# Rectify and sum rows of 1024: two of seven large loads issued from ScalarE's queue, with other step lengths for two of them

## The chip, the core and the metric

The kernel runs on one core of one Trainium2 chip. The time is the device time of one execution in microseconds (us), and the median of three runs is compared. The core has engines that work side by side, each with its own instruction stream[...]: here ScalarE (ACT in the profile), VectorE (DVE) and SyncE (SP), which computes nothing and issues transfers. TensorE has no work, and GpSimd (POOL) only sets four constants at the start. Sixteen DMA engines carry the transfers between memory (HBM) and the core's own memory of 128 partitions.

## The reference

```python
def reference(x):                       # x: 32 x 512 x 1024, float32
    relu_x = np.maximum(x, 0)
    return np.sum(relu_x, axis=-1).astype(np.float32)    # 32 x 512
```

There are 16,384 rows of 1024 numbers, 67.1 MB in all. Of each row the positive numbers are summed.

## The kernel before

The rows are dealt to 128 partitions, 128 rows to each. The tile `buf` holds three buffers of 16 rows per partition (64 KB per partition, 8 MB in all), and `res` the 128 sums of each partition.

The input comes in seven chunks of 16 rows per partition (`CHUNKS`, c0 to c6), then in a tail of smaller loads: 8, 4 and 2 rows (`TAIL`), and the last two rows in four pieces. c0 consists of a load of one row and one of fifteen. Each of c1 to c6 is one load whose piece in each partition is 64 KB of contiguous memory. Chunk c goes to buffer c mod 3.

All loads are issued by SP, in order, at L91 (chunks), L101 (`TAIL`), L112 and L115 (last pieces), on one queue. The first three chunks go out at once. From c3 on, L87 makes SP wait until VectorE has finished with the chunk that held the buffer: `done[c]` is the number of VectorE's reductions up to the end of chunk c, and `s_dve` counts them. So c3 waits for `done[0]`, c4 for `done[1]`, c5 for `done[2]`, c6 for `done[3]`, and the tail for `done[4]`. Each load counts up its own semaphore `s_in[c]` when it lands.

Chunks c0 to c5 are worked by two engines one after the other (loop at L138). ScalarE waits for `s_in[c]`, then rectifies the chunk in place (L145) in steps of so many rows as `ACT_STEPS[c]` says, each counting `s_act`. VectorE sums the rectified rows (L160) in steps of `DVE_STEPS[c]` rows; each step waits for the first of ScalarE's steps that cover all its rows. Two reductions can thus wait for two different steps of one chunk. Where the steps of ScalarE cover fewer than 16 rows (c5: 12), the other four are `alone` rows: ScalarE does two and VectorE two, each rectifying and summing in one instruction (`on_act` L127, `on_dve` L130). After c1 a small transpose (L169) prepares the first 128 sums for storing.

c6 and the tail are not split into two stages: there the engines take rows in turn with `on_act` and `on_dve`, so each row is done by one instruction. The last sums are then stored by SP (L207), and the program ends when they are in memory.

Of the kernel before, what the change touches and what calls it, by code (L numbers as in the profile page):

```python
# [6 lines left out]
NB = 3  # L7
REGIONS = [1, 111, 16]
CHUNKS = [[(0, 0, 1), (1, 0, 15)]] + [[(1, 16 * c + 15, 16)] for c in range(6)]
ACT_STEPS = [[16], [7, 9], [7, 9], [7, 9], [4, 5, 7], [3, 4, 5]]  # L10
DVE_STEPS = [[4, 5, 7], [7, 4, 5], [7, 4, 5], [7, 4, 5], [4, 5, 7], [3, 4, 5]]
TAIL = [8, 4, 2]
CUT = 912
HEAD = 256
# [2 lines left out]
def bass_relu_sum_kernel(  # L17
    nc: bass.Bass,
    x: bass.AP,
    out: bass.AP,  # L20
):

# [20 lines left out]
    xv = [  # L45
        xr[P * s : P * (s + n), :].rearrange("(p j) d -> p j d", p=P)
        for s, n in zip(start, REGIONS)
    ]
    ov = [of[P * s : P * (s + n)].rearrange("(p j) -> p j", p=P) for s, n in zip(start, REGIONS)]

    buf = nc.alloc_sbuf_tensor("buf", [P, NB, BIG, D], fp32)
# [6 lines left out]
    s_in = [nc.alloc_semaphore(f"s_in{i}") for i in range(n_in)]  # L58
    s_act = nc.alloc_semaphore("s_act")
    s_dve = nc.alloc_semaphore("s_dve")  # L60
# [9 lines left out]
    sp, act, dve = nc.sync, nc.scalar, nc.vector  # L70

    NTWO = len(ACT_STEPS)
    done = [sum(map(len, DVE_STEPS[: c + 1])) for c in range(NTWO)]

# [8 lines left out]
        if ins.engine == mybir.EngineType.SP and type(ins).__name__ == "InstDrain"  # L83
    )
    for c in range(NBIG + 1):
        if c >= NB:
            sp.wait_ge(s_dve, done[c - NB])  # L87
        if c < NBIG:
            i = 0
            for g, j, n in CHUNKS[c]:  # L90
                sp.dma_start(  # L91
                    out=buf[:, c % NB, i : i + n, :], in_=xv[g][:, j : j + n, :]
                ).then_inc(s_in[c], 16)
                i += n
                if c == 0:
                    code.insert(arrival, code.pop())
                    arrival += 1
# [13 lines left out]
    for k, (lo, hi) in enumerate((first, second, third)):  # L111
# [6 lines left out]
        out=of[0:P].rearrange("(k q) -> k q", q=32), in_=turned[0:P:32, 0:32]  # L118
# [7 lines left out]
    def on_act(t, acc):  # L126
        return act.activation(t, t, AF.Relu, accum_out=acc)  # L127

    def on_dve(t, acc):
        return dve.tensor_scalar(  # L130
            out=t, in0=t, scalar1=0.0, scalar2=None, op0=ALU.max, op1=ALU.add, accum_out=acc
        )

    def row(c, i):
        return buf[:, c % NB, i, :], res[:, c * BIG + i : c * BIG + i + 1]

    k = 0
    for c in range(NTWO):  # L138
        alone = BIG - sum(ACT_STEPS[c])
        act.wait_ge(s_in[c], 16 * len(CHUNKS[c]))  # L140
        r = 0
        ready = []
        for n in ACT_STEPS[c]:
            t = buf[:, c % NB, r : r + n, :]
            act.activation(t, t, AF.Relu).then_inc(s_act, 1)  # L145
            k += 1
            ready += [k] * n
            r += n
        for i in range(BIG - alone // 2, BIG):
            on_act(*row(c, i))  # L150
        if alone:
            dve.wait_ge(s_in[c], 16 * len(CHUNKS[c]))
            for i in range(BIG - alone, BIG - alone // 2):
                on_dve(*row(c, i))
        r = seen = 0
        for n in DVE_STEPS[c]:
            if ready[r + n - 1] > seen:
                seen = ready[r + n - 1]
                dve.wait_ge(s_act, seen)
            dve.tensor_reduce(  # L160
                out=res[:, c * BIG + r : c * BIG + r + n],
                in_=buf[:, c % NB, r : r + n, :],
                axis=X,
                op=ALU.add,
            ).then_inc(s_dve, 1)
            r += n
        if c == 1:
            dve.wait_ge(s_dve, done[c])
            dve.transpose(out=turned[:, :], in_=res[:, 0:32]).then_inc(s_turn, 1)  # L169
# [68 lines left out]
```

## Time and profile before

| | |
|---|---|
| median of three runs | 160.91 us (160.76 to 160.96) |
| the profiled execution | 160.74 us |
| its span in the profile | 159.4 us |
| bytes moved | 67.18 MB, mean 421 GB/s |
| ScalarE's wait for the first chunk | 19.1 us |
| VectorE's wait for ScalarE's first step | 35.5 us |
| ScalarE's waits for all six chunks | 46.1 us |
| last store, issue to landing | 1.4 us |

The span is what the profiler saw of the program, and 1.34 us of the measured time lie around it. In the profile a line begins with the place in the code (L160), then comes the engine, the operation, what it writes and reads, and how often. A row of the timeline begins with start and duration in us; at its end stands the idle time before it and what ended that. `SPq` is SP's issuing of a transfer[...]; the transfer itself runs on the DMA engines. A digit of a row of slices is the busy share of one fortieth of the span in tenths. Queue `q1` is the one that SP issues on.

### The profile page before, as it was taken

Reading aid. Unit: us, or ns where it says so; the run is one execution under the profiler, and the core shown is the slowest. Engines: PE = TensorE matmul, PEld = TensorE weight load, DVE = VectorE, ACT = ScalarE, POOL = GpSimd, SP = SyncE. Lnnn points to the kernel's source line nnn. Section 1 sums busy time; section 2 is a strip of 40 time slices with the busy share of each in tenths; the row PEclk is TensorE's granted clock in tenths of the full one; section 3 lists DMA queues with packets and bytes.
Section 4 is the critical chain, followed back from the end, with each engine's and each line's share of the span. In section 5 each row is a group of like instructions: output and inputs, shape, how many; then the busy total and the mean of one; then the engine's idle time right before and its main releaser. Section 6 shows DMA issues by size and latency. Waiting matters only on the chain.

```text
span 159.4 us, 150 instructions
## 1 busy us (share of the span) xinstructions
DVE 120.6 (76%) x59; ACT 101.5 (64%) x54; POOL 0.2 (0%) x4
## 2 busy tenths in 40 slices
DVE  0000000009999999999999999999999999898995
ACT  3000059980799708996099941999329980496975
POOL 0000000000000000000000000000000000000000
DMA  9997996996996997989979969969969979798994
GB/s 378 493 401 339 493 526 263 526 526 263 526 493 296 526 444 345 526 378 411 526 312 477 526 263 526 526 263 526 526 263 526 444 345 526 321 469 374 417 400 142
DMA packets 2457, 67.18 MB, mean 421 GB/s; under 512 B 536, under 2 KB 792, under 8 KB 1176
## 3 DMA queue, kind: packets, MB, share of 16 engines
q1 hardware_dynamic: 2456, 67.18, 98.1%
q14 instruction: 1, 0.01, 0.0%
HBM read 67.11 MB, written 0.07 MB: 421 GB/s over the span
## 4 chain that ended last, share of the span: by engine, by line
DVE 55%; DMA 34%; ACT 9%; SPq 2%; issue 0%
DVE res L160 54%; DMA buf<-in_x_dram 34%; ACT buf L145 9%; SPq L101 1%; SPq L112 1%; DVE buf L130 0%; DVE seam L130 0%; SPq L91 0%; DVE turned L169 0%
## 5 line engine op out<-in xcount | busy, mean ns | idle before, releaser
L160 DVE TENSOR_REDUCE res<-buf 128x4 f32<-128x4096 f32 (+3 forms) x18 | 99.4, 5596 | 35.5 <-ACT buf L145 35.5
L145 ACT ACTIVATE buf<-buf 128x7168 f32<-128x7168 f32 (+5 forms) x13 | 80.4, 6233 | 46.1 <-DMA buf<-in_x_dram 46.1
L127 ACT ACTIVATE buf<-buf 128x1024 f32<-128x1024 f32 (+2 forms) x19 | 19.0, 999 | 8.9 <-DMA buf<-in_x_dram 8.9
L130 DVE TENSOR_SCALAR_CACHE_REDUCE buf<-buf 128x1024 f32<-128x1024 f32 (+2 forms) x19 | 20.7, 1143 | 1.7 <-DMA buf<-in_x_dram 1.6
L127 ACT ACTIVATION_READ_ACCUMULATOR buf<-buf 128x1 f32 x19 | 3.6, 188 | 0.0
L145 ACT ACT_TABLE_LOAD x1 | 1.3, 1283 | 1.3 <-PEq L223 1.3
L130 DVE DVE_READ_ACCUMULATOR buf<-buf 128x1 f32 x19 | 1.6, 84 | 0.0
L130 DVE TENSOR_SCALAR_CACHE_REDUCE seam<-seam 128x258 f32<-128x258 f32 x1 | 0.4, 421 | 0.0
L127 ACT ACTIVATE seam<-seam 128x114 f32<-128x114 f32 x1 | 0.3, 300 | 0.1
L169 DVE STREAM_TRANSPOSE turned<-res 128x32 f32<-128x32 f32 x1 | 0.2, 211 | 0.0
L127 ACT ACTIVATION_READ_ACCUMULATOR seam<-seam 128x1 f32 x1 | 0.2, 186 | 0.0
L223 POOL MEMSET const-bfloat16-1.0<- 128x1 bf16 x1 | 0.1, 101 | 0.0
L223 POOL MEMSET const-uint8-127<- 128x1 uint8 x1 | 0.1, 101 | 0.0
L223 POOL MEMSET const-float32-0.0<- 128x1 f32 x1 | 0.1, 98 | 0.2 <-issue 0.2
L223 POOL MEMSET const-float32-1.0<- 128x1 f32 x1 | 0.1, 98 | 0.0
L130 DVE DVE_READ_ACCUMULATOR seam<-seam 128x1 f32 x1 | 0.1, 82 | 0.0
## 6 DMA issues: line engine op xcount, KB each, us to landing
buf<-in_x_dram SPq DMA_DIRECT2D x1, 7680.0 KB, 21.1
buf<-in_x_dram SPq DMA_DIRECT2D x1, 4096.0 KB, 25.3
buf<-in_x_dram SPq DMA_DIRECT2D x1, 2048.0 KB, 29.9
buf<-in_x_dram SPq DMA_DIRECT2D x1, 1024.0 KB, 31.9
buf<-in_x_dram SPq DMA_DIRECT2D x1, 512.0 KB, 3.3
buf<-in_x_dram SPq DMA_DIRECT2D x1, 456.0 KB, 32.5
buf<-in_x_dram SPq DMA_DIRECT2D x1, 256.0 KB, 32.7
seam<-in_x_dram SPq DMA_DIRECT2D x1, 184.0 KB, 32.6
```

What stands on the lines that cost most here:

```text
L101: sp.dma_start(out=buf[:, tb, r : r + n, :], in_=xv[-1][:, r : r + n, :]).then_inc(s_in[NBIG + i], 16)
L112: sp.dma_start(out=flat[:, lo:hi], in_=rows[:, lo:hi]).then_inc(s_in[NBIG + len(TAIL) + k], 16)
L127: return act.activation(t, t, AF.Relu, accum_out=acc)
L130: return dve.tensor_scalar(out=t, in0=t, scalar1=0.0, scalar2=None, op0=ALU.max, op1=ALU.add, accum_out=acc)
L145: act.activation(t, t, AF.Relu).then_inc(s_act, 1)
L160: dve.tensor_reduce(out=res[:, c * BIG + r : c * BIG + r + n], in_=buf[:, c % NB, r : r + n, :], axis=X, op=ALU.add,).then_inc(s_dve, 1)
L169: dve.transpose(out=turned[:, :], in_=res[:, 0:32]).then_inc(s_turn, 1)
L223: nc = _bacc.Bacc("TRN2", target_bir_lowering=False, num_devices=1)
```

## The change

The loads of c3 and c5 (the fourth and the sixth chunk) are no longer issued by SP but by ScalarE, on its own queue. SP's loop leaves them out, its wait with them. In ScalarE's stream the load of chunk c + 2 stands after the rectifying steps of chunk c: c3's after those of c1, c5's after those of c3. Each has the same condition as before, a wait for `done[c - 1]` of the loop (`done[0]` for c3, `done[2]` for c5), and counts the same semaphore at landing. c4, c6 and the tail remain with SP and their waits.

The steps of two chunks change. c3 is rectified in one step of 16 rows instead of two (7 and 9); c4 in two (7, 9) instead of three (4, 5, 7). VectorE's steps for c3 and c4 are exchanged accordingly. The number of reductions in each chunk stays three, so `done` keeps its values, and the work done on each row stays the same.

```diff
-ACT_STEPS = [[16], [7, 9], [7, 9], [7, 9], [4, 5, 7], [3, 4, 5]]
-DVE_STEPS = [[4, 5, 7], [7, 4, 5], [7, 4, 5], [7, 4, 5], [4, 5, 7], [3, 4, 5]]
+ACT_STEPS = [[16], [7, 9], [7, 9], [16], [7, 9], [3, 4, 5]]
+ON_ACT = (3, 5)
+DVE_STEPS = [[4, 5, 7], [7, 4, 5], [7, 4, 5], [4, 5, 7], [7, 4, 5], [3, 4, 5]]
...
     for c in range(NBIG + 1):
+        if c in ON_ACT:
+            continue
         if c >= NB:
             sp.wait_ge(s_dve, done[c - NB])
...
             k += 1
             ready += [k] * n
             r += n
+        if c + 2 in ON_ACT:
+            [(g, j, n)] = CHUNKS[c + 2]
+            act.wait_ge(s_dve, done[c - 1])
+            act.dma_start(out=buf[:, (c + 2) % NB, :, :], in_=xv[g][:, j : j + n, :]).then_inc(
+                s_in[c + 2], 16
+            )
         for i in range(BIG - alone // 2, BIG):
             on_act(*row(c, i))
```

## The prediction

> **What bounds the kernel now.** I read the page's busy shares and slices first, then the chain of waits, then the timelines of SP's queue, ScalarE and VectorE, then the groups by shape.[...]
>
> ```profile
> span 159.4 us, 150 instructions
> DVE 120.6 (76%) x59; ACT 101.5 (64%) x54; POOL 0.2 (0%) x4
> DVE  0000000009999999999999999999999999898995
> ACT  3000059980799708996099941999329980496975
> q1 hardware_dynamic: 2456, 67.18, 98.1%
> ...
> 35.50 34.59 DVE res L160 x6
> 70.09 0.02 issue
> 70.11 0.21 DVE turned L169
> 70.33 51.73 DVE res L160 x9
> ...
> DVE buf L130 <- DMA buf<-in_x_dram: 1.6, 4, 0.5
> ```
>
> Two resources are full together. The 16 DMA engines carry packets for 98.1% of the span, and VectorE, once its first input is there at 35.50, works almost without a hole: the chain runs through its reductions for 86 us, and all its later waits sum to 1.6 us. So a hole of more than 1.6 us opened in VectorE after 35.5 us lengthens the run one for one, even if no byte comes later.
>
> ```profile
> 52.86 0.33 SPq L91 DMA_DIRECT2D buf<-in_x_dram  x1
> 70.11 0.33 SPq L91 DMA_DIRECT2D buf<-in_x_dram  x1
> 87.58 0.33 SPq L91 DMA_DIRECT2D buf<-in_x_dram  x1
> ...
> 40.97 13.95 ACT L145 ACTIVATE buf<-buf 128x7168 f32<-128x7168 f32 x2 [5.50 <-DMA buf<-in_x_dram]
> 60.31 13.95 ACT L145 ACTIVATE buf<-buf 128x7168 f32<-128x7168 f32 x2 [5.39 <-DMA buf<-in_x_dram]
> 79.67 13.95 ACT L145 ACTIVATE buf<-buf 128x7168 f32<-128x7168 f32 x2 [5.41 <-DMA buf<-in_x_dram]
> 99.02 14.04 ACT L145 ACTIVATE buf<-buf 128x4096 f32<-128x4096 f32 x3 [5.40 <-DMA buf<-in_x_dram]
> ...
> L160 DVE TENSOR_REDUCE res<-buf 128x7 f32<-128x7168 f32 x5 | 37.9, 7605 | 0.0
> L160 DVE TENSOR_REDUCE res<-buf 128x5 f32<-128x5120 f32 x6 | 32.9, 5480 | 0.0
> L160 DVE TENSOR_REDUCE res<-buf 128x4 f32<-128x4096 f32 x6 | 26.5, 4413 | 35.5 <-ACT buf L145 35.5
> L145 ACT ACTIVATE buf<-buf 128x16384 f32<-128x16384 f32 x1 | 13.9, 13856 | 19.1 <-DMA buf<-in_x_dram 19.1
> ```
>
> The SP lines are the issues of c3, c4 and c5. ScalarE starts each chunk when it lands, so its lines give the landings: c1 40.97, c2 60.31, c3 79.67, c4 99.02, one every 19.35 us. c3 is issued at 52.86, while c2 still has 7.4 us to go: on one queue it stands behind c2 and costs it nothing. A chunk is 64 KB in each of 128 partitions, eight per DMA engine, so one 64-KB piece takes 19.35/8 = 2.42 us.
>
> [...] (2)[...] 8.389 MB per 19.35 us is 433.5 GB/s, so a second queue has nothing left to win. (3)[...] No run here shows it yet; both cases are worked out.[...]
>
> **The change part by part.**
>
> 1. c3 moves to ScalarE's queue. With (3) it goes out at 52.86 as before, on done[0]. Start-up: the first 512 KB landed 3.3 us after issue, of which 0.5 MB at 433 GB/s is 1.2, so 2.1 us lie at both ends; I take 1.5 of it before the first byte (estimate), which makes 54.4. c2's pieces run from 60.2 - 19.35 = 40.85; at 54.4 its sixth is under way and ends at 55.4. Then in turns: c3's first to 57.8, c2's seventh to 60.2, c3's second to 62.6, c2's eighth to 65.0. c2 lands at 65.1 instead of 60.31.
>
> 2. c4 goes out on SP's queue at done[1], unmoved at 70.1; bytes from 71.6. c3 has been alone since 65.0 and its fifth piece ends at 72.3. Then c4, c3, c4, c3, c4, c3: the eighth of c3 ends at 72.3 + 6 x 2.42 = 86.8, and it lands at 87.0 instead of 79.67. That is three pieces, 7.3 us.
>
> 3. VectorE in c2: ScalarE's first step is done at 65.1 + 6.17 = 71.3, its second (7.87) at 79.2. VectorE is free at 70.33, waits 1.0, reduces seven rows to 78.9, waits 0.3, then 4.41 + 5.48 to 89.1 (before 87.58).
>
> 4. c3's rectifying becomes one step of 16 rows. Nothing can be reduced until all of it is done: 87.0 + 13.86 = 100.9. VectorE idles from 89.1 to 100.9, 11.8 us. Before, the seven-row step sufficed, 79.67 + 6.17 = 85.8, ahead of 87.58. The joining saves one ACTIVATE's fixed cost:[...] 13.95 against 13.86, so 0.09 us.
>
> 5. VectorE's holes: 1.0 + 0.3 + 11.8 = 13.1 us, against slack of 1.6: **+11.5 us**. The new orders (4,5,7 for c3, 7,4,5 for c4) sum to the same 17.5 us a chunk, cost nothing.
>
> 6. c5 on ScalarE's queue, and c4's steps [7,9]. c5 goes out at done[2] = 89.1 and shares with c4: bytes 90.7, turns from 91.7; c4 ends at 106.2, lands at 106.3 (before 99.02). ScalarE has its first step ready at 112.5 and its second at 120.4; VectorE, in c3 until 100.9 + 17.5 = 118.4, needs them at 118.4 and 126.0: hidden. c5's rest ends at 118.3.
>
> 7. c6 stays on SP, on done[3], now 118.4 instead of 104.8: bytes at 119.9, a DMA hole of 1.6 us; c6 lands near 139.4. The tail goes out at done[4], 135.9, before c6 is in. VectorE comes to c6 only at 150.4 to 151.0 (137.30, the end of its last c5 reduction, plus 13.1 to 13.7, as much as the sum of step 5 and the shift of done[3], 104.8 to 118.4, say), so all later landings are hidden by its own lateness. If c6 were later by over 11 us this would matter.
>
> 8. Two DMA issues on ScalarE's sequencer, 0.33 us each by SP's rows. What stands behind each is the next chunk's activation, which waits for a landing 8 us or more away: nothing.
>
> If instead the DMA waits until the activation before it has ended (against (3)): c3 out at 40.97 + 13.95 = 54.9, bytes at 56.5, inside c2's seventh piece; c2 lands at 62.7 and no longer holds VectorE, but c3 still ends at 86.8. VectorE idles from 87.6 to 100.9, 13.3 us, the same sum. c5 then goes out at 100.9 and the DMA stands for 3.5 us after c4's end at 98.9, hidden under VectorE's lateness, as in step 7. The time hardly tells the two apart.
>
> Sum: the profiled execution took 160.74 (span 159.4 and 1.34 around it). 160.74 + 11.5 = 172.2; the median of the runs, 160.91, is 0.17 above: **172.4**.
>
> Bounds of the unknown sharing: from below, no sharing at all (first come, first served). c3 lands at 79.67, is rectified at 93.5, VectorE waits from 87.6 to 93.5, 5.9 - 1.6 = +4.3: 165.2. Nothing lower while the rate stands: c2 and c3 together can't be in before 79.4, and if c3 is not the last of them, c2 is, and VectorE waits for it sooner and longer. From above, c3 goes first whenever it can: c3 in at 74, c2 last at 79.6, first reduction at 85.8 instead of 70.3: 15.5, and after it c3's step, ready at 107.4 against done[2] at 103.1, 4.3 more: +18.2, 179.
>
> **The rivals.**
>
> A, even turns, c3 three pieces late: 172.4. For it: 64-KB pieces standing in both queues[...].
> B, pieces of the old queue already taken in when the new one begins go first, so that c3 is one or two late: 165.2 + 2.42 or 4.84, 167.6 to 170.0.[...]
> C, whole loads in order of arrival: 165.2, all of it from the sixteen-row step.[...]
> D, ScalarE's queue gets more than half, or c3 is four pieces late: 174.8 to 179.
> E, not slower: two queues fill gaps that one leaves, so bytes come faster from 54 us on. It decides from the point where c3 is in by 87.58 + 1.6 - 13.86 = 75.3: 25 us of transfer in 20.9, 520 GB/s, with VectorE's floor 160.9 - 1.6 = 159.3. The slices of the page show single values near 526, but next to 263, so they are bookkeeping; the mean of 421 and (2) speak against it. 159.3 to 160.9.
>
> **How the numbers follow.** A 0.64, B 0.13, C 0.14, D 0.06, E 0.03. The likeliest gives 172.4. The range must take in C and B and an error of one piece above A (2.42): 164.8 to 175.0, with most of D and E left out. A measurement of this kernel tells 0.2% from no change; E is split 0.02 faster, 0.01 same, the rest is slower: 0.97.
>
> **What would show it.** Right: ScalarE starts c2 near 65 and c3 near 87; VectorE has one hole of 11 to 13 us ended by ScalarE's sixteen-row step near 101, none worth naming after it; one DMA queue more, holding 16.8 MB; the tail's waits for DMA gone from VectorE. If c2 starts at 60.3 and c3 at 79.7, C holds. If c5 goes out near 89, the sequencer ran ahead; near 101, it did not. Wrong altogether: c3 in by 75, or c2's landing past 70.

## The result, and the profile after

The changed kernel takes 171.97 us (median of four runs, 171.94 to 172.02) against 160.86 us before (four runs as well): a ratio of 1.069 (95% interval 1.068 to 1.071). The profiled execution took 171.97 us, with a span of 170.6 us. The forecast was 172.4 us in a range of 164.8 to 175.0.

These are lines of the page of the changed kernel, and below the dots its waits by engine (time in all, number of times, longest). Its lines L95, L149, L170 and L134 are L91, L145, L160 and L130 of before.

```profile
span 170.6 us, 148 instructions
DVE 120.5 (71%) x59; ACT 101.2 (59%) x52; POOL 0.2 (0%) x4
DVE  0000000069999999799980039999999999999996
ACT  3000099934998007995069960999999109987500
q1 hardware_dynamic: 2168, 50.40, 69.4%
q10 hardware_dynamic: 288, 16.78, 22.7%
...
DVE res L170 <- ACT buf L149: 48.6, 4, 35.5
```

VectorE is busy for as long as before (120.5 against 120.6 us) and the same bytes move, now 16.78 MB of them on a second queue, `q10`. The difference is a hole in VectorE's row of slices, the digits 80039, and a DMA share that fell from 98.1% to 92.1%. VectorE now waits four times for ScalarE instead of once, 48.6 us instead of 35.5: 13.1 us more. Its waits for the tail's loads, 1.6 us before, have gone from the list.

The timelines of the changed kernel, VectorE's above and ScalarE's below the dots (start, duration, what; in brackets the idle time before it and what ended that; `ACTq` is ScalarE's issuing of a load):

```profile
70.07 0.21 DVE L179 STREAM_TRANSPOSE turned<-res 128x32 f32<-128x32 f32 x1
71.39 7.62 DVE L170 TENSOR_REDUCE res<-buf 128x7 f32<-128x7168 f32 x1 [1.11 <-ACT buf L149]
79.16 9.81 DVE L170 TENSOR_REDUCE res<-buf 128x4 f32<-128x4096 f32 x2 [0.15 <-ACT buf L149]
100.84 34.58 DVE L170 TENSOR_REDUCE res<-buf 128x4 f32<-128x4096 f32 x6 [11.87 <-ACT buf L149]
...
52.83 0.38 ACTq L156 DMA_DIRECT2D buf<-in_x_dram  x1
65.18 13.95 ACT L149 ACTIVATE buf<-buf 128x7168 f32<-128x7168 f32 x2 [10.29 <-DMA buf<-in_x_dram]
86.95 13.86 ACT L149 ACTIVATE buf<-buf 128x16384 f32<-128x16384 f32 x1 [7.82 <-DMA buf<-in_x_dram]
89.01 0.33 ACTq L156 DMA_DIRECT2D buf<-in_x_dram  x1
106.30 24.47 ACT L149 ACTIVATE buf<-buf 128x7168 f32<-128x7168 f32 x5 [5.50 <-DMA buf<-in_x_dram]
```

Read ScalarE first. c2 starts at 65.18 instead of 60.31, c3 at 86.95 instead of 79.67, c4 at 106.30 instead of 99.02. c3 is rectified in one step of 13.86 us, so nothing of it can be summed before 100.81. VectorE is out of c2 at 88.97 and starts c3 at 100.84. After that it never waits again. The chain of waits of the changed kernel says the same in order of time:

```profile
52.83 34.10 DMA buf<-in_x_dram
86.93 0.02 issue
86.95 13.87 ACT buf L149
100.82 0.02 issue
100.84 34.58 DVE res L170 x6
```

The load of c3 alone, 34.1 us from issue to landing, carries the chain here. In the kernel before, the 86 us in the middle of the chain were VectorE's without a break.

### The profile page after: what moved, and what is told of

Read it like the earlier page. It is cut to its first block, busy times and chain, and to the rows that moved or that the text cites. A ratio compares the mean times of both kernels' runs of the same rounds, so it can differ in the third digit from the quotient of the medians.

```text
span 170.6 us, 148 instructions
## 1 busy us (share of the span) xinstructions
DVE 120.5 (71%) x59; ACT 101.2 (59%) x52; POOL 0.2 (0%) x4
## 3 DMA queue, kind: packets, MB, share of 16 engines
q10 hardware_dynamic: 288, 16.78, 22.7%
## 4 chain that ended last, share of the span: by engine, by line
DMA 43%; DVE 40%; ACT 15%; issue 0%
DMA buf<-in_x_dram 43%; DVE res L170 28%; ACT buf L149 15%; DVE buf L134 12%; DVE seam L134 0%
## 5 line engine op out<-in xcount | busy, mean ns | idle before, releaser
L170 DVE TENSOR_REDUCE res<-buf 128x4 f32<-128x4096 f32 (+3 forms) x18 | 99.7, 5596 | 48.6 <-ACT buf L149 48.6
L149 ACT ACTIVATE buf<-buf 128x7168 f32<-128x7168 f32 (+5 forms) x11 | 80.1, 7331 | 48.1 <-DMA buf<-in_x_dram 48.1
L134 DVE TENSOR_SCALAR_CACHE_REDUCE buf<-buf 128x1024 f32<-128x1024 f32 (+2 forms) x19 | 20.4, 1136 | 0.0
L134 DVE DVE_READ_ACCUMULATOR buf<-buf 128x1 f32 x19 | 1.5, 79 | 0.0
L134 DVE TENSOR_SCALAR_CACHE_REDUCE seam<-seam 128x258 f32<-128x258 f32 x1 | 0.4, 421 | 0.0
L134 DVE DVE_READ_ACCUMULATOR seam<-seam 128x1 f32 x1 | 0.1, 82 | 0.0
```

What stands on the lines that cost most here:

```text
L134: return dve.tensor_scalar(out=t, in0=t, scalar1=0.0, scalar2=None, op0=ALU.max, op1=ALU.add, accum_out=acc)
L170: dve.tensor_reduce(out=res[:, c * BIG + r : c * BIG + r + n], in_=buf[:, c % NB, r : r + n, :], axis=X, op=ALU.add,).then_inc(s_dve, 1)
```

## The experiments

All runs are of the changed kernel with the edit shown, except where the old step lengths are put back. Each was timed beside the kernel before on the same chip.

**Step lengths alone.**

```diff
-ON_ACT = (3, 5)
+ON_ACT = ()
```

> All loads on SP's queue again, only the new step lengths kept. Theory of turns (A): without a second queue c3 lands at 79.7 as before; the sixteen-row step ends at 93.5 and VectorE, free at 87.6, waits 5.9 us; less 1.6 us of slack gives 164.7 to 165.2. If instead the long step itself cost nothing and all the loss came from the second queue, 160.9.

165.12 us, ratio 1.026 (1.024 to 1.028). VectorE's timeline of this kernel:

```profile
70.24 17.30 DVE L170 TENSOR_REDUCE res<-buf 128x7 f32<-128x7168 f32 x3
93.54 34.58 DVE L170 TENSOR_REDUCE res<-buf 128x4 f32<-128x4096 f32 x6 [6.00 <-ACT buf L149]
```

There is one new hole, 6.00 us, at the place and of the size that the long step should give, with every landing where it was before. So part of the loss has nothing to do with queues.

**Second queue alone.**

```diff
-ACT_STEPS = [[16], [7, 9], [7, 9], [16], [7, 9], [3, 4, 5]]
+ACT_STEPS = [[16], [7, 9], [7, 9], [7, 9], [4, 5, 7], [3, 4, 5]]
...
-DVE_STEPS = [[4, 5, 7], [7, 4, 5], [7, 4, 5], [4, 5, 7], [7, 4, 5], [3, 4, 5]]
+DVE_STEPS = [[4, 5, 7], [7, 4, 5], [7, 4, 5], [7, 4, 5], [4, 5, 7], [3, 4, 5]]
```

> c3 and c5 on ScalarE's queue, the old step lengths. Theory A: ScalarE starts c2 at 65.2 and c3 at 87.0 as in the changed kernel, but its seven-row step is done at 93.1, so VectorE waits 1.1 + 0.2 + 4.1 us instead of 13.1; 5.4 less 1.6 gives about 164.6. If the steps carried the whole loss, 160.9; if the queue carried nearly all of it, 170 or more.

164.83 us, ratio 1.024 (1.022 to 1.025). VectorE's timeline:

```profile
71.40 7.62 DVE L170 TENSOR_REDUCE res<-buf 128x7 f32<-128x7168 f32 x1 [1.05 <-ACT buf L149]
79.17 9.81 DVE L170 TENSOR_REDUCE res<-buf 128x4 f32<-128x4096 f32 x2 [0.15 <-ACT buf L149]
93.17 7.62 DVE L170 TENSOR_REDUCE res<-buf 128x7 f32<-128x7168 f32 x1 [4.18 <-ACT buf L149]
100.94 27.07 DVE L170 TENSOR_REDUCE res<-buf 128x4 f32<-128x4096 f32 x5 [0.15 <-ACT buf L149]
```

c3 lands at 86.95 here too, but its first seven rows are ready at 93.1. Step lengths and queue cost 4.2 and 3.9 us alone (the kernel before took 160.93 us beside them) and 11.1 together. The surplus has a plain reason: the kernel before had two reserves that each half could use by itself, 1.6 us of VectorE's slack and the 1.7 us by which c3's first step (85.8) was ahead of VectorE (87.6). Together they can be spent only once: 4.2 + 3.9 + 1.6 + 1.7 is 11.4, against 11.1 measured.

**Loads that wait for ScalarE's own work.** One line is added ahead of the load in ScalarE's stream:

```diff
+            act.wait_ge(s_act, k)
             act.wait_ge(s_dve, done[c - 1])
```

> The changed kernel, but each load on ScalarE's queue waits for ScalarE's own earlier steps to end, so c3 goes out at 54.9 and c5 at 100.8 instead of 52.8 and 89.0. Theory (the sequencer's running ahead is worth nothing here): DMA stands about 3 us after c4, but VectorE comes to c6 only at 150, so 172.0, unchanged within 0.5. Rival: the hole in the transfers adds to the time, 174 to 176.

172.17 us, ratio 1.070 (1.068 to 1.071). The two issues moved to 55.01 and 100.87, and VectorE's one hole came to 13.26 us, ending at 100.87:

```profile
55.01 0.39 ACTq L157 DMA_DIRECT2D buf<-in_x_dram  x1
62.80 13.95 ACT L149 ACTIVATE buf<-buf 128x7168 f32<-128x7168 f32 x2 [7.82 <-DMA buf<-in_x_dram]
86.98 13.86 ACT L149 ACTIVATE buf<-buf 128x16384 f32<-128x16384 f32 x1 [10.24 <-DMA buf<-in_x_dram]
100.87 0.33 ACTq L157 DMA_DIRECT2D buf<-in_x_dram  x1
```

c2 comes 2.4 us sooner and c3 at the same moment as in the changed kernel, so the two small holes in c2 melt into the large one. An issue of c5 that is 12 us later is hidden by VectorE's lateness. Whether the loads go out during ScalarE's steps or after them makes little difference to the time (171.97 against 172.17 us).

**One of the two loads at a time.** `ON_ACT` is `(3,)` in the first run, `(5,)` in the second.

> Only c3 on ScalarE's queue; c5 is SP's again; new step lengths. Theory A: c5's place costs nothing since VectorE's hole is closed at 100.8 by c3 alone: 172.0, c4 landing at 99.0 again instead of 106.3. Rival: half of the loss belongs to c5's sharing with c4, about 166.

172.22 us, ratio 1.070 (1.068 to 1.071): with the new step lengths, c3's move by itself makes the whole loss. c4 is no longer held up (the DMA records have it in by 98.8 us), and that buys nothing.

> Only c5 on ScalarE's queue; c3 is SP's again; new step lengths. c3 lands at 79.7, the long step opens 5.9 us as with the steps alone (165.1); then c4 shares with c5 and lands at 106 to 109, its seven-row step is done at 112.5 to 115, VectorE is out of c3 at 111.0 and waits 1.5 to 4 more: 167 to 169. Rival: c5's move is free wherever it stands, 165.1.

169.25 us, ratio 1.052 (1.051 to 1.054), a little above the 167 to 169 us that were expected. VectorE's timeline:

```profile
93.64 17.34 DVE L170 TENSOR_REDUCE res<-buf 128x4 f32<-128x4096 f32 x3 [6.02 <-ACT buf L149]
114.97 7.62 DVE L170 TENSOR_REDUCE res<-buf 128x7 f32<-128x7168 f32 x1 [3.99 <-ACT buf L149]
```

So c5's move isn't harmless in itself: it delays c4 (ScalarE starts it at 108.76, with the step lengths alone at 99.00) as c3's delays c2, and costs 4.1 us over the step lengths alone. In the changed kernel it is free only because VectorE has already been made late enough by c3.

**How the DMA engines share.** Now the pieces of one of two loads that share the engines are made small. A chunk loaded as four loads of 4 rows has pieces of 16 KB instead of 64 KB; bytes, buffers and waits stay. First c3, on ScalarE's queue (its load becomes a loop over the four parts, issued one after the other):

```diff
+CHUNKS[3] = [(1, 16 * 2 + 15 + i, 4) for i in range(0, 16, 4)]
```

> The changed kernel with c3 as four loads of 4 rows, so 16-KB pieces against SP's 64-KB pieces; same bytes, same moments. If the DMA engines take turns by piece: c2 is hardly held up (lands near 61.6), but c3 gets a fifth of the rate beside c4 and lands near 99: ScalarE's long step ends near 113, about 184. If they share by bytes: c2 65, c3 87, 172.

184.61 us, ratio 1.148 (1.146 to 1.150). ScalarE's timeline, and below the dots the line of VectorE that waits for it:

```profile
61.55 13.95 ACT L150 ACTIVATE buf<-buf 128x7168 f32<-128x7168 f32 x2 [6.63 <-DMA buf<-in_x_dram]
99.25 13.86 ACT L150 ACTIVATE buf<-buf 128x16384 f32<-128x16384 f32 x1 [23.75 <-DMA buf<-in_x_dram]
...
113.14 34.59 DVE L173 TENSOR_REDUCE res<-buf 128x4 f32<-128x4096 f32 x6 [25.59 <-ACT buf L150]
```

c3 is late by 12.3 us more than in the changed kernel, with the same bytes issued from the same moment on (52.87). The turns here went by piece, with 16 KB as with 64 KB: beside c4 the DMA records have one small piece (0.61 us), then one large (2.42 us), and so on, so of every 80 KB c3 got 16, a fifth. A sharing by bytes, for which c3 was expected at 87, is excluded by its start at 99.25.

Then the other way round: c3 whole on ScalarE's queue, SP's c4 in small pieces, with the new and with the old step lengths.

```diff
-ON_ACT = (3, 5)
+ON_ACT = (3,)
+CHUNKS[4] = [(1, 16 * 3 + 15 + i, 4) for i in range(0, 16, 4)]
```

> Only c3 on ScalarE's queue, in 64-KB pieces; SP's c4 as four loads of 4 rows, 16-KB pieces. By piece: c2 as in the changed kernel, 65.2; c3 holds four fifths beside c4 and lands near 81.6 instead of 87.0, the long step ends at 95.5, VectorE waits 1.1 + 0.2 + 6.4: 166.5. By bytes: 172.

166.84 us, ratio 1.037 (1.036 to 1.039); c3 lands at 81.67 and the hole before it is 6.52 us. Only c4's pieces differ from the run with c3 alone on the second queue (172.22 us, c3 at 87.08).

> As the run before, with the old step lengths. By piece: c3 lands near 81.6, its seven-row step is done at 87.8, before VectorE is out of c2 at 89.0, so all that is left is 1.3 us of waiting in c2, within the slack: 161.0, the same as the kernel before. By bytes: 164.8, as with the queue alone.

161.13 us, ratio 1.003 (1.002 to 1.005). ScalarE's timeline, then VectorE's:

```profile
65.21 13.95 ACT L150 ACTIVATE buf<-buf 128x7168 f32<-128x7168 f32 x2 [10.29 <-DMA buf<-in_x_dram]
81.61 13.95 ACT L150 ACTIVATE buf<-buf 128x7168 f32<-128x7168 f32 x2 [2.45 <-DMA buf<-in_x_dram]
...
71.42 7.62 DVE L171 TENSOR_REDUCE res<-buf 128x7 f32<-128x7168 f32 x1 [1.08 <-ACT buf L150]
79.19 44.30 DVE L171 TENSOR_REDUCE res<-buf 128x4 f32<-128x4096 f32 x8 [0.15 <-ACT buf L150]
```

With c3 on the second queue, but in the larger of the two pieces, it lands at 81.61 instead of 86.95, and nearly all of the loss is gone; 0.3% stays, and no gain appears. Besides c4's pieces, this run differs from that with the queue alone (164.83 us) by c5, which is SP's again; but there VectorE never waited in c4, so c5 is not the difference. So in these runs it isn't ScalarE's queue as such that costs (161.13 us with c3 on it), but how its load and the one on the other queue share the engines. The DMA engines were 98.1% full before, and none of these runs beat the kernel before.

**What holds a load in ScalarE's stream.** The run with c3 in small pieces held a surprise: c5 went out at 99.26, 11.7 us after the reductions that it waits for. In the next run c5's load stands ahead of c3's long step; all else is as in that run.

```diff
+        if c + 2 in ON_ACT and c == 3:
+            act.wait_ge(s_dve, done[c - 1])
+            i = 0
+            for g, j, n in CHUNKS[c + 2]:
+                act.dma_start(
...
         act.wait_ge(s_in[c], 16 * len(CHUNKS[c]))
...
-        if c + 2 in ON_ACT:
+        if c + 2 in ON_ACT and c < 3:
```

> As the run with c3 in 16-KB pieces, but c5's load stands before c3's long step in ScalarE's stream. In that run c5 went out at 99.26, at the moment c3 landed and the step in front of it began, though the reductions that it waits for were done at 87.57. If an activation whose semaphore is not there yet holds what stands behind it, c5 now goes out near 87.6; if ScalarE's sequencer had been free and something else held the load, it stays near 99. Since c5 stands behind c3 on the queue, c3 still lands near 99.3 and the time stays near 184.6.

184.50 us, ratio 1.147 (1.145 to 1.150), and the issue moved as the first alternative said. ScalarE's timeline of the first and then of the second of these kernels:

```profile
99.25 13.86 ACT L150 ACTIVATE buf<-buf 128x16384 f32<-128x16384 f32 x1 [23.75 <-DMA buf<-in_x_dram]
99.26 0.33 ACTq L158 DMA_DIRECT2D buf<-in_x_dram  x1
```

```profile
87.69 0.34 ACTq L149 DMA_DIRECT2D buf<-in_x_dram  x1
99.36 19.92 ACT L158 ACTIVATE buf<-buf 128x16384 f32<-128x16384 f32 x2 [23.77 <-DMA buf<-in_x_dram]
```

So in these runs a load passed an activation that was running (89.01 in the changed kernel, during the step from 86.95 to 100.81), but not one whose semaphore was still missing (99.26, with the step's start at 99.25). That something on the queue held it is excluded: in the second kernel it went out at 87.69, while c3's four loads were still under way (ScalarE starts c3 at 99.36). What in ScalarE held it, the runs don't show.

**One sum for all runs.** VectorE's waits for ScalarE after its first start, less the 1.57 us of slack that the kernel before had at its end, against the measured difference of the profiled executions (160.74 before):

| run | new waits | less 1.57 | measured |
|---|---|---|---|
| changed kernel | 13.13 | 11.6 | 11.2 |
| step lengths alone | 6.00 | 4.4 | 4.3 |
| queue alone | 5.53 | 4.0 | 4.1 |
| loads wait for ScalarE | 13.26 | 11.7 | 11.5 |
| c3 alone | 13.17 | 11.6 | 11.5 |
| c5 alone | 10.16 | 8.6 | 8.6 |
| c3 in small pieces | 25.59 | 24.0 | 23.7 |
| c4 in small pieces | 7.70 | 6.1 | 6.1 |
| the same, old steps | 1.23 | -0.3 | 0.4 |
| c3 in small pieces, c5's load ahead | 25.59 | 24.0 | 23.8 |

With c4 in small pieces and the old steps the slack isn't used up: 0.6 us of waiting for the tail is left, and -0.3 + 0.6 is 0.3.

## Why the prediction was right, point by point

Step 1 said that c2 lands at 65.1, and it landed at 65.18, yet two terms in it were off by one piece each and cancelled. The DMA records of the changed kernel show it (start of the first and last record of a turn, queue, bytes, number of engines; us from the span's start):

```
52.35-52.75  q1   65536  x16   c2, sixth piece
54.78-55.18  q1   65536  x16   c2, seventh
57.20-57.59  q10  65536  x16   c3, first
59.62-60.01  q1   65536  x16   c2, eighth
62.03-62.42  q10  65536  x16   c3, second
64.45-64.84  q1       4  x16   c2, completion
64.45-64.84  q10  65536  x16   c3, third
```

c3's first piece came at 57.2 and not at 55.4: one more piece of the old queue ran first. The start-up of 1.5 us doesn't explain it. Where the DMA engines stood idle, the first pieces started 0.95 to 1.56 us after the issue (c6 of the changed kernel, issued at 118.21) and 0.97 to 1.85 us (c5 in the run whose loads wait, issued at 100.87), so by these figures c3 was ready before the turn at 54.78 (an estimate). And seven engines gave c3 still another turn at 74.12, 4.1 us after c4's issue. Why, the records don't show; they show the order.

c2's last byte was therefore in at 62.0 to 62.4, not at 65.0. But on each engine `q1` has a record of four bytes at 64.45 to 64.84, 2.42 us after c2's last byte, with a whole piece of c3 between. In the kernel before it came with no piece between (c2's last byte in at 59.43 to 59.92, the four bytes at 59.42 to 59.92, ScalarE's start at 60.31). ScalarE starts c1, c2, c3 and c4 of the changed kernel 0.34 to 0.40 us after the last of their four-byte records (40.59, 64.84, 86.57, 105.90), so these are read here as the report of the finished load. So the landing came at 65.18.

The sum was right with a mistaken list of terms, and that the two mistakes cancelled was luck. Rival B's order was there, one more piece of the old queue ahead of the new one (54.78 before 57.20); that pieces are taken in ahead, as B had it, was not shown. On the slowest engines c3's bytes were two pieces late, not three (the last byte in by 84.16, before by 79.30). Without the report's turn the same working would have put c3's landing near 84.5 and the time near 170 us, the upper end of B. (This is an estimate: c3's last byte was in by 84.16, and ScalarE started about 0.35 us after the last report; 84.5 + 13.86 less 87.58 is a hole of 10.8 us, less 1.57 of slack.)

Step 2 (c3 at 87.0) came out at 86.95 by the same two corrections, and so did step 6 (c4 at 106.3): c5's first piece came at 93.46, and c4's report at 105.54, one piece of c5 after its last byte. On seven of the sixteen engines c3's last piece started at 78.95 and its report at 83.79; on the other nine, where c4 had the first turn, at 81.39 and 86.22, and ScalarE started c3 at 86.95, after the last of these nine.

Steps 3 and 4, VectorE's waits and the long step, were 1.0 + 0.3 + 11.8 and are 1.11 + 0.15 + 11.87. Step 5, the sum: the waits are 13.13 against 13.1, and the time 171.97 against 172.2 before the median's 0.17 was added. The waits would make it 172.3; the 0.3 us that it came out lower lie partly in VectorE's last rows, 20.4 us of instructions in place of 20.7. Steps 6 and 7: c4 at 106.3 and c6's issue at 118.4 are 106.30 and 118.21; c6 landed at 140.45 instead of 139.4, and VectorE, which came to it only at 150.60, didn't wait for it. The bound of 79.4 us for c2 and c3 together is 79.6 by the prediction's own figures (40.85 + 2 x 19.35); nothing hung on it.

Step 8 and the alternative after it: the second load went out at 89.01, during the step that stands ahead of it (86.95 to 100.81), so ScalarE's sequencer ran ahead of the running step, and the run that forbids it took nearly the same time (172.17). That a load need not wait until the activation ahead of it has ended was (3) of the prediction, an assumption that no trace of before shows. It held for an activation that was running. Behind one that still waited for its semaphore the load was held: 99.26 against 87.69. The first load's issue at 52.83 doesn't bear on this, since of the two activations ahead of it one had ended and the other was running from 47.0 on.

Of the rivals, first come, first served (C) is refuted by c2 at 65.18; the long step's 4.3 us that made up all of it are confirmed, by the run with the steps alone. B's times, 167.6 to 170.0, were missed because of the reports. A larger share for ScalarE's queue (D) is refuted by the records, in which the two queues alternate piece by piece (57.20, 59.62, 62.03). That they take turns was an assumption of the prediction, since before had one loading queue; the traces show it. Turns of several pieces they don't show: while both queues had pieces, and once the later load had its first, the turn passed on after every single one, of 64 KB (2.42 us) or of 16 (0.61 us). A gain from a second queue (E) is refuted as well: pieces of c3 and c4 in turns take 2.42 us each, as on one queue, so (2) of the prediction, an estimate from the rate on one queue, held.

## What to carry to other kernels

Here the DMA engines were full (98.1% of the span), and a second queue brought no bytes (2.42 us a piece, as before); it let a later load push in among the pieces of an earlier one, and the earlier was needed first. Before moving a load, write down when each engine needs each chunk: VectorE was free for c2 at 70.33, ScalarE's first step takes 6.17, so c2 had to be in by 64.2, and with c3 among its pieces it came at 65.18.

A longer step in the first of two stages saved 0.09 us here (13.86 against 13.95), and made the second stage wait for all 16 rows instead of seven, 7.7 us more. The lead of 1.7 us that c3 had before hid a part of that price; once the load was late, it showed in full.

## What the runs showed of the hardware that was not expected

- The load on the second queue did not get the next turn: c3 went out at 52.83 and, by an estimate from the start-ups seen on idle engines (0.95 to 1.85 us), was ready before the turn at 54.78, but had its first piece only at 57.2, after one more piece of c2.
- The report of a finished load came a turn later than its last byte: on each engine 2.42 us lie between c2's last byte and its report, beside 64-KB pieces on the other queue. Of the 4.9 us by which c2 landed later than before, half is a piece of c3 ahead of its last piece, and half is its report. The queue with the smaller pieces got the smaller share: c3 in pieces of 16 KB lands at 99.25 instead of 86.95, and c2 beside them at 61.55 instead of 65.18.
- In these runs a load behind an activation on ScalarE went out while that activation ran (89.01, during the step from 86.95 to 100.81), but was held as long as the activation waited for its semaphore (99.26 instead of 87.69).
